# Attention scores of two heads from one 128-row product, with the keys of the pair beside zeros

## The chip, the cores and the metric

One core of one Trainium2 chip runs the whole kernel. The metric is the time of one execution in device microseconds (us). A core has five engines that run side by side, each through its own instructions in order: TensorE (PE in the profile, its weight loads as PEld), VectorE (DVE), ScalarE (ACT), GpSimd (POOL) and SyncE (SP), which here issues nearly all the DMA transfers.

## The reference

Two layers over 256 tokens of width 1024. Each layer is a gated feed-forward block (FFN), a mixer with attention, and a second FFN; each of the three is normed before and after and modulated by vectors computed from `c`.

```python
def reference(x, c, ...):
    c_act = jax.nn.silu(c)
    for l in range(DEPTH):                       # DEPTH = 2
        mod = (c_act @ ada_w[l] + ada_b[l])[:, None, :]
        sh1, sc1, g1, sh2, sc2, g2, sh3, sc3, g3 = jnp.split(mod, N_MOD, axis=-1)
        h = rmsnorm(x, norm_pre[l, 0]) * (1.0 + sc1) + sh1
        y = swiglu(h, ffn_w_gate[l, 0], ffn_w_up[l, 0], ffn_w_down[l, 0])
        x = x + 0.5 * g1 * rmsnorm(y, norm_post[l, 0])
        h = rmsnorm(x, norm_pre[l, 1]) * (1.0 + sc2) + sh2
        y = hybrid_mixer(h, mix_w_in[l], mix_b_in[l], mix_w_out[l], attn_sinks[l], group_gain[l], rel_bias)
        x = x + g2 * rmsnorm(y, norm_post[l, 1])
        ...                                      # a second FFN, as the first
    return x
```

The mixer projects `h` to queries, keys and values. Eight heads of width 64 attend within a window of 128 tokens (here "window heads": two groups of four query heads share the keys and values of one of two key heads). Eight further heads have keys and values of their own and, at 256 tokens, attend causally to all of them ("block heads"). For every head the scores are `q @ k.T * 64**-0.5` plus a bias that depends on the distance, masked; then a softmax, and the product with the values. Both groups are normed, joined and projected back.

## The kernel before

Tokens lie in two halves of 128, h = 0 and h = 1. Names that end in `_a` belong to half 0 (or an even step), in `_b` to half 1. Weights come from HBM in units of 1 MB: SP loads a unit into one of three `raw` buffers, ACT rounds it into one of six `hi` buffers (L442), DVE writes the rest, raw minus hi, into one of five `lo` buffers (L443), and PE multiplies three times (hi by hi, hi by lo, lo by hi) in a fast fp32 format: `mm3` (L481 to L483, 512 columns) and `mm3t` (here L489 to L491, 256 columns). A weight buffer is free again when PE has read it for the last time. The vectors from `c` are summed on DVE beside this (L506).

Attention itself is computed in plain fp32. One plain fp32 product is two records of PE in the trace, each with its own weight load. A mixer (`mixer`, one for each half) makes the keys and queries of the window heads from rows (transposed by `turn`, L709, into `kTw` and `qTa`), and those of the block heads with `cols_of` (L716), which writes them transposed, two heads on top of each other in the 128 partitions, into a tile of 128x512. `quad_attn` (L764) then takes four heads: two biases are loaded from a table by SP (`toeplitz`), four score products of 64 rows are issued (L778: 64 partitions of the contraction, 128 columns for half 0, 256 for half 1), into two PSUM tiles, one for the heads of the upper 64 partitions (j = 0) and one for those of the lower (j = 1):

```python
            for i in range(2):
                for j in range(2):
                    hf = slice(j * HD, (j + 1) * HD)
                    ...
                    nc.tensor.matmul(sp[j][:, i, :ncol], q_, k_, start=True, stop=True)
```

DVE adds the bias and takes the row's maximum (L783), ACT takes the exponential (L788), PE transposes it (L794), ACT copies the transposed block out of PSUM (L796), and PE multiplies it with the values (L803). In a layer and half there are four such calls, so 16 heads; over both layers 64 products of 128 columns and 64 of 256, which is 128 records of 64x128 and 64x256 in the trace (two for each of 32 heads and halves, counted by shape: 64 and 64).

The order is not that of the code: `keep_order` (L77) gathers all instructions, plays them through with its own table of costs (`cost`, L51) and priorities, and then fixes for each engine the order that came out. Weight and staging buffers go to the tiles in program order, as buffers become free. PSUM tiles of the kind `w` (`wps`) come in two buffers for each half.

Of the kernel before, what the change touches and what calls it, by code (L numbers as in the profile page):

```python
# [10 lines left out]
F32 = mybir.dt.float32  # L11
# [4 lines left out]
P = 128  # L16
# [9 lines left out]
NV = 384  # L26

NRAW, NARAW, NHI, NLO = 3, 2, 6, 5
NST, NSTR, NBIAS, NBROW, NACC, NROW = 3, 10, 3, 2, 2, 5
START_MM, START_CONV, START_CHAIN, START_SMALL = 590, 826, -286, 74  # L30
START_ORDER = ['s0 x0 s1 c0 g0 x1 c1 f0 s2 f1', 'c2 g1 f2 s3 c3 f3', '', '', '']
WARM = [2, 5, 2]
# [263 lines left out]
def trunk(ctx, tc, x, c, rel_bias, ada_w, ada_b, norm_pre, norm_post, w_gate, w_up,  # L296
# [57 lines left out]
    def ctile(shape, name, dt=F32):  # L354
        return cp.tile(shape, dt, tag=name, name=name)
# [346 lines left out]
            if (l, i) != (DEPTH - 1, 2):  # L702
                pre_norm(h, *((l, 1) if i == 0 else (l + 1, 0)))

    kTw = ctile([P, S], "kTw")
    vw = [ctile([P, P], f"vw{h}") for h in range(2)]
    kv = {}

    def turn(src, n, dst, scale):  # L709

        p_ = wps()
        for t in range(n):
            nc.tensor.transpose(p_[:, t * P:(t + 1) * P], src[:, t * P:(t + 1) * P], ident)
        nc.scalar.activation(dst, p_.rearrange("p (a b) -> p a b", a=4)[:, :n, :], AF.Copy, scale=scale)

    def cols_of(l, c0, scale):  # L716

        p_ = wps()
        w = u_cols(l, c0, 1)
        t0 = (c0 - 768) // P  # L720
        dst = stage()
        for t in range(2):
            for k in range(KT):
                mm3t(p_[:, t * 256:(t + 1) * 256], k, w, slice(t * P, (t + 1) * P), k == 0, k == KT - 1)
            nc.scalar.activation(dst[:, t * 256:(t + 1) * 256], p_[:, t * 256:(t + 1) * 256], AF.Identity,
                                 scale=scale, bias=bq[:, l, t0 + t:t0 + t + 1])
        return dst

    def mixer(h, l):

        nk = 1 + h
        toks = slice(h * P, (h + 1) * P)

        def brow(c0, n):
            return bcast(b_in[l:l + 1, c0:c0 + n], n)


        p_ = wps()
        w = u_cols(l, 512, 2)
        for k in range(8):  # L740
            mm3(p_[:, :256], hT[0][:, h, k, :], hT[1][:, h, k, :], w, k, slice(0, 256), k == 0, k == 7)
        b_ = brow(512, 256)
        ks = st()
        nc.vector.tensor_add(ks[:, :P], p_[:, :P], b_[:, :P])
        nc.vector.tensor_add(vw[h], p_[:, P:256], b_[:, P:])
        turn(ks, 1, kTw[:, toks].rearrange("p (o t) -> p o t", o=1), 1.0)

        p_ = wps()
        rows_of(h, [p_], [lambda q: u_in(l, 0, q)])
        qs = st()  # L750
        nat = lambda t: t.rearrange("p (j i d) -> p j i d", j=2, i=4)
        nc.vector.tensor_tensor(qs.rearrange("p (i j d) -> p j i d", i=4, j=2), nat(p_), nat(brow(0, 512)), op=ALU.add)
        qTa = stage()
        turn(qs, 4, qTa.rearrange("p (a b) -> p a b", a=4), 0.125)
        yield

        p_ = wps()
        rows_of(h, [p_], [lambda q: u_in(l, 1792, q)])
        kv["v", h] = stage()
        nc.vector.tensor_add(kv["v", h], p_, brow(1792, 512))  # L760

        negm, lsum = tiny(16, f"negm{h}"), tiny(16, f"lsum{h}")

        def quad_attn(i0, swa, acc):  # L764

            head = (lambda j, i: 4 * j + i) if swa else (lambda j, i: 8 + 2 * i + j)
            ncol = nk * P
            bt = [toeplitz(head(j, i0), head(0, 1) - head(0, 0), ncol) for j in range(2)]
            sp = [wps().rearrange("p (i k) -> p i k", i=2) for _ in range(2)]
            for i in range(2):  # L770
                for j in range(2):
                    hf = slice(j * HD, (j + 1) * HD)
                    if swa:
                        q_, k_ = qTa[hf, (i0 + i) * P:(i0 + i + 1) * P], kTw[hf, :ncol]
                    else:
                        q_ = kv["q", i0 // 2][hf, i * 256 + h * P:i * 256 + (h + 1) * P]
                        k_ = kv["k", i0 // 2][hf, i * 256:i * 256 + ncol]
                    nc.tensor.matmul(sp[j][:, i, :ncol], q_, k_, start=True, stop=True)  # L778
            s = [st().rearrange("p (a b) -> p a b", a=2) for _ in range(2)]
            for j in range(2):  # L780
                for i in range(2):
                    hd_ = head(j, i0 + i)
                    nc.vector.tensor_tensor_reduce(s[j][:, i, :ncol], sp[j][:, i, :ncol], bt[j][:, i, :ncol], -1.0,  # L783
                                                   nsink[:, l, hd_:hd_ + 1] if swa else 3.0e38, ALU.add, ALU.min,
                                                   negm[:, hd_:hd_ + 1])
                for i in range(2):
                    hd_ = head(j, i0 + i)
                    nc.scalar.activation(s[j][:, i, :ncol], s[j][:, i, :ncol], AF.Exp, scale=-1.0, bias=negm[:, hd_:hd_ + 1],  # L788
                                         accum_out=lsum[:, hd_:hd_ + 1])
                tp = wps()  # L790
                for i in range(2):
                    for b in range(nk):
                        t = i * nk + b
                        nc.tensor.transpose(tp[:, t * P:(t + 1) * P], s[j][:, i, b * P:(b + 1) * P], ident)  # L794
                pT = st()
                nc.scalar.activation(pT[:, :2 * ncol], tp[:, :2 * ncol], AF.Copy)  # L796
                for i in range(2):
                    hd_ = head(j, i0 + i)
                    vc = j * HD if swa else (hd_ - 8) * HD
                    oc = (hd_ % 8) * HD  # L800
                    for b in range(nk):
                        t = i * nk + b
                        nc.tensor.matmul(acc[:, oc:oc + HD], pT[:, t * P:(t + 1) * P], (vw[b] if swa else kv["v", b])[:, vc:vc + HD],  # L803
                                         start=b == 0, stop=b == nk - 1)

        def group_out(g, acc):
            hs = slice(g * 8, g * 8 + 8)
            if g == 0:
                e = tiny(8, f"es{h}")
                nc.vector.tensor_add(e, sinkb[:, l, :], negm[:, hs])  # L810
                nc.scalar.activation(e, e, AF.Exp)
                nc.vector.tensor_add(lsum[:, hs], lsum[:, hs], e)
            rl = tiny(8, f"rl{h}")
            nc.vector.reciprocal(rl, lsum[:, hs])
            y = st()
            nc.vector.tensor_tensor(y.rearrange("p (a b) -> p a b", a=8), acc.rearrange("p (a b) -> p a b", a=8),
                                    rl.rearrange("p (a o) -> p a o", o=1).to_broadcast([P, 8, HD]), op=ALU.mult)
            ss = tiny(1, f"ssg{h}")
            nc.scalar.activation(junk, y, AF.Square, scale=512.0 ** -0.5, accum_out=ss)
            r2 = rstd_of(ss, None, "rstdg")  # L820
            y2 = st()
            nc.vector.scalar_tensor_tensor(y2, y, r2, bcast(group_gain[l:l + 1, g * 512:(g + 1) * 512], 512),
                                           op0=ALU.mult, op1=ALU.mult)
            to_T(h, g * 4, 4, y2)

        yield
        acc0 = aps(h)
        quad_attn(0, True, acc0)
        yield
        quad_attn(2, True, acc0)  # L830
        yield
        acc1 = aps(h)
        quad_attn(0, False, acc1)
        yield
        group_out(0, acc0)
        yield
        quad_attn(2, False, acc1)
        yield
        group_out(1, acc1)
        yield  # L840
        accs = [aps(h), aps(h)]
        for u in range(4):
            w = u_out(l, u)
            for n in range(2):
                for k in range(2):
                    kt = u * 2 + k
                    mm3(accs[n], hT[0][:, h, kt, :], hT[1][:, h, kt, :], w, k, slice(n * 512, (n + 1) * 512),
                        kt == 0, kt == 7)
        yield
        post_norm(h, l, 1, accs)  # L850
        pre_norm(h, l, 2)

    def mix(l):
        steps = [mixer(h, l) for h in range(2)]

        def go(h):
            cur[0] = h
            next(steps[h], None)

        for step in sec["mix"]:  # L860
            if step < "2":
                go(int(step))
            else:
                cur[0] = 0
                g = int(step) - 2
                kv["k", g] = cols_of(l, 1280 + g * 256, 1.0)
                kv["q", g] = cols_of(l, 768 + g * 256, 0.125)


    def first_srcs(q):  # L870
# [156 lines left out]
```

## Time and profile before

| | |
|---|---|
| time, median of 3 runs | 1036.47 us (1036.47 to 1038.14) |
| the profiled execution | 1035.72 us, of which its span 1033.9 us from the first to the last instruction |
| PE busy, share of the span | 98%, 6578 products |
| PE weight loads | 87% |
| DVE, ACT, POOL busy | 78%, 53%, 4% |
| DMA | 263.9 MB through SP's queue, 76% of 16 engines' span |

The span is the profiled execution's own; 1.8 us lie around it. A record of PE has a start that was measured and an end that is modelled, and records overlap: how long PE takes for one is read from its start to the start of the next. The two attention stretches lie at about 230 to 330 us (layer 0) and 725 to 830 us (layer 1), the FFNs in between and around them.

### The profile page before, as it was taken

How to read it: one execution, taken by the hardware profiler on the slowest of the kernel's cores; microseconds unless marked ns; L12 is line 12 of the kernel's file. 1: busy time of each engine (PE TensorE's matmuls, PEld its weight loads, DVE VectorE, ACT ScalarE, POOL GpSimd, SP SyncE). 2: the span in 40 equal slices, each digit the busy share in tenths (PEclk: the TensorE clock that was granted, in tenths of full speed). 3: DMA queues.
4: the chain of work that ended last, by engine and by line, in shares of the span. 5: the costliest groups of instructions: out<-in, count | busy, mean ns of one | idle time of the engine just before them, and what ended most of it. 6: DMA issues, size and time to landing. Idle time of an engine off the chain costs nothing.

```text
span 1033.9 us, 17402 instructions
## 1 busy us (share of the span) xinstructions
PE 1017.8 (98%) x6578; PEld 902.0 (87%) x6578; DVE 802.2 (78%) x1493; ACT 546.3 (53%) x1238; POOL 38.4 (4%) x74
## 2 busy tenths in 40 slices
PE   8999999999999999999999999999999999999997
PEld 3699998978888899999979999998888879999996
DVE  4799887988887998888888988786878698554542
ACT  2456434565667655556465445454566666444431
POOL 1000000020001000000010000000000110000000
PEclk9999999999999999999999999999999999999999
DMA  9999999969885587989838998885688647556511
GB/s 328 362 350 325 319 306 362 333 212 285 309 287 167 190 302 258 319 291 311 285 121 293 324 315 302 281 305 182 201 298 279 186 150 262 204 168 200 174 71 41
DMA packets 173919, 265.10 MB, mean 256 GB/s; under 512 B 6412, under 2 KB 109548, under 8 KB 173836
## 3 DMA queue, kind: packets, MB, share of 16 engines
q1 hardware_dynamic: 173680, 263.93, 76.0%
q8 instruction: 51, 0.84, 0.3%
q14 instruction: 32, 0.26, 0.1%
q10 hardware_dynamic: 156, 0.07, 0.0%
HBM read 262.90 MB, written 4.22 MB: 258 GB/s over the span
## 4 chain that ended last, share of the span: by engine, by line
issue 56%; PE 33%; DMA 4%; DVE 3%; POOL 2%; ACT 1%; SPq 1%; POOLq 0%; DVEq 0%; ACTq 0%
PE w_a L489 3%; PE w_a L491 3%; PE w_a L490 3%; PE a_b L481 2%; PE a_b L482 2%; PE a_b L483 2%; DMA raw_a<-in_ffn_w_up_dram 2%; PE w_b L778 2%; PE a_b L803 1%; PE a_a L481 1%; PE a_a L482 1%; PE a_a L483 1%; PE w_a L778 1%; DMA araw_a<-in_ada_w_dram 1%; PE w_b L482 1%
## 5 line engine op out<-in xcount | busy, mean ns | idle before, releaser
L443 DVE TENSOR_TENSOR lo_a<-raw_a,hi_a 128x512 fp32r<-128x512 f32 (+1 forms) x540 | 294.2, 594 | 48.9 <-issue 23.4
L442 ACT ACTIVATE hi_a<-raw_a 128x512 fp32r<-128x512 f32 (+1 forms) x540 | 259.5, 547 | 129.9 <-DMA raw_a<-in_ffn_w_up_dram 26.1
L489 PE MATMUL w_a<-hTh,hi_a 128*128 128x256 f32 x768 | 218.7, 285 | 1.1 <-ACT hi_a L442 1.1
L490 PE MATMUL w_a<-hTl,hi_a 128*128 128x256 f32 x768 | 217.6, 284 | 0.0
L491 PE MATMUL w_a<-hTh,lo_a 128*128 128x256 f32 x768 | 217.5, 284 | 0.0
L489 PEld LDWEIGHTS w_a<-hTh,hi_a 128*128 128x128 f32 x768 | 147.2, 192 | 2.4 <-ACT hi_a L442 1.3
L490 PEld LDWEIGHTS w_a<-hTl,hi_a 128*128 128x128 f32 x768 | 147.2, 192 | 0.8
L491 PEld LDWEIGHTS w_a<-hTh,lo_a 128*128 128x128 f32 x768 | 146.9, 192 | 0.3
L490 PE MATMUL w_b<-hTl,hi_b 128*128 128x256 f32 x512 | 145.0, 283 | 0.0
L489 PE MATMUL w_b<-hTh,hi_b 128*128 128x256 f32 x512 | 144.9, 283 | 0.0
L491 PE MATMUL w_b<-hTh,lo_b 128*128 128x256 f32 x512 | 144.8, 283 | 0.0
L443 DVE TENSOR_TENSOR lo_b<-raw_b,hi_b 128x512 fp32r<-128x512 f32 (+1 forms) x224 | 120.3, 590 | 24.7 <-issue 17.5
L442 ACT ACTIVATE hi_b<-raw_b 128x512 fp32r<-128x512 f32 (+1 forms) x224 | 105.6, 544 | 64.0 <-PE w_b L490 27.0
L489 PEld LDWEIGHTS w_b<-hTh,hi_b 128*128 128x128 f32 x512 | 98.1, 192 | 1.1
L490 PEld LDWEIGHTS w_b<-hTl,hi_b 128*128 128x128 f32 x512 | 98.1, 192 | 0.9
L491 PEld LDWEIGHTS w_b<-hTh,lo_b 128*128 128x128 f32 x512 | 98.0, 192 | 0.2
L506 DVE SCALAR_TENSOR_TENSOR acc_a<-araw_a,ccol,acc_a 128x512 f32<-128x512 f32 x110 | 82.4, 749 | 7.8 <-DMA araw_a<-in_ada_w_dram 6.2
L482 PE MATMUL a_b<-lo_a,str_a 128*128 128x512 f32 x156 | 60.8, 392 | 0.0
L483 PE MATMUL a_b<-hi_a,str_a 128*128 128x512 f32 x156 | 60.4, 390 | 0.0
L481 PE MATMUL a_b<-hi_a,str_a 128*128 128x512 f32 x156 | 59.7, 391 | 0.0
L506 DVE SCALAR_TENSOR_TENSOR acc_b<-araw_b,ccol,acc_b 128x512 f32<-128x512 f32 x46 | 34.5, 749 | 7.9 <-DMA araw_b<-in_ada_w_dram 7.1
L481 PE MATMUL w_a<-hi_a,hTh 128*128 128x512 f32 (+1 forms) x96 | 36.1, 378 | 0.6 <-DVE hTl L591 0.6
(240 smaller groups left out, 1732.7 us busy)
## 6 DMA issues: line engine op xcount, KB each, us to landing
araw_a<-in_ada_w_dram SPq DMA_DIRECT2D x84, 512.0 KB
raw_a<-in_ffn_w_down_dram SPq DMA_DIRECT2D x30, 1024.0 KB
raw_a<-in_ffn_w_gate_dram SPq DMA_DIRECT2D x26, 1024.0 KB
raw_a<-in_ffn_w_up_dram SPq DMA_DIRECT2D x26, 1024.0 KB
araw_b<-in_ada_w_dram SPq DMA_DIRECT2D x44, 512.0 KB
raw_a<-in_mix_w_in_dram SPq DMA_DIRECT2D x18, 1024.0 KB
raw_b<-in_ffn_w_gate_dram SPq DMA_DIRECT2D x16, 1024.0 KB
raw_b<-in_ffn_w_up_dram SPq DMA_DIRECT2D x16, 1024.0 KB
```

Source lines behind the costliest of these rows:

```text
L442: nc.scalar.activation(hi[:, sl], raw[:, sl], AF.Copy)
L443: nc.vector.tensor_sub(lo[:, sl], raw[:, sl], hi[:, sl].bitcast(F32))
L481: nc.tensor.matmul(ps_, hh, wh, start=start, stop=False)
L482: nc.tensor.matmul(ps_, hh, wl, start=False, stop=False)
L483: nc.tensor.matmul(ps_, hl, wh, start=False, stop=stop)
L489: nc.tensor.matmul(ps_, wh, hh, start=start, stop=False)
L490: nc.tensor.matmul(ps_, wh, hl, start=False, stop=False)
L491: nc.tensor.matmul(ps_, wl, hh, start=False, stop=stop)
L506: nc.vector.scalar_tensor_tensor(acc[:, :n], raw[:, t, :], ccol[:, k:k + 1], b if t == 0 else acc[:, :n], op0=ALU.mult, op1=ALU.add)
L778: nc.tensor.matmul(sp[j][:, i, :ncol], q_, k_, start=True, stop=True)
L803: nc.tensor.matmul(acc[:, oc:oc + HD], pT[:, t * P:(t + 1) * P], (vw[b] if swa else kv["v", b])[:, vc:vc + HD], start=b == 0, stop=b == nk ...
```

## The change

The score products of a pair of heads become one product of 128 rows. The keys of the pair stand in a tile with two column blocks for each pair: in the first block the 64 upper partitions hold the keys of head j = 0 and the lower are zero, in the second the lower hold those of j = 1 and the upper are zero. The queries of both heads (128 partitions) are the stationary operand, both blocks (256 or 512 columns) move, and the result has the scores of both heads side by side in one PSUM tile. The rest of the attention then goes pair by pair. The zeros of the window heads' tile `kzw` are written once at the start; the block heads' tile is taken from the pool of `hi` buffers in each layer, and POOL writes its zeros there each time. ACT writes the keys in two halves. The staging pool `str` goes from 10 buffers to 9. Line numbers of the changed kernel are higher by 17 in its attention: the products of the scores stand at L796, the transposes at L811, the value products at L820.

```diff
-NST, NSTR, NBIAS, NBROW, NACC, NROW = 3, 10, 3, 2, 2, 5
+NST, NSTR, NBIAS, NBROW, NACC, NROW = 3, 9, 3, 2, 2, 5
...
-    kTw = ctile([P, S], "kTw")
+    kzw = ctile([P, 2, S], "kzw")
+    nc.gpsimd.memset(kzw[HD:, 0, :], 0.0)
+    nc.gpsimd.memset(kzw[:HD, 1, :], 0.0)
...
-    def cols_of(l, c0, scale):
+    def cols_of(l, c0, scale, dst):
...
-            nc.scalar.activation(dst[:, t * 256:(t + 1) * 256], p_[:, t * 256:(t + 1) * 256], AF.Identity,
-                                 scale=scale, bias=bq[:, l, t0 + t:t0 + t + 1])
-        return dst
+            for rows_, to in dst(t):
+                nc.scalar.activation(to, p_[rows_, t * 256:(t + 1) * 256], AF.Identity,
+                                     scale=scale, bias=bq[rows_, l, t0 + t:t0 + t + 1])
+
+    def keys_of(l, g):
+
+        if g == 0:
+            t = phi.tile([P, 2048], F32, tag="hi", name=nm("kz"))
+            kv["k"] = t.rearrange("p (i j n) -> p i j n", i=4, j=2)
+            nc.gpsimd.memset(kv["k"][HD:, :, 0, :], 0.0)
+            nc.gpsimd.memset(kv["k"][:HD, :, 1, :], 0.0)
+        kz = kv["k"]
+        cols_of(l, 1280 + g * 256, 1.0, lambda t: [(slice(j * HD, (j + 1) * HD), kz[j * HD:(j + 1) * HD, g * 2 + t, j, :])
+                                                   for j in range(2)])
...
-        turn(ks, 1, kTw[:, toks].rearrange("p (o t) -> p o t", o=1), 1.0)
+        kt_ = turn(ks, 1)
+        for j in range(2):
+            hf = slice(j * HD, (j + 1) * HD)
+            nc.scalar.activation(kzw[hf, j, toks], kt_[hf, :], AF.Copy)
...
-            bt = [toeplitz(head(j, i0), head(0, 1) - head(0, 0), ncol) for j in range(2)]
-            sp = [wps().rearrange("p (i k) -> p i k", i=2) for _ in range(2)]
-            for i in range(2):
+            for i in range(i0, i0 + 2):
+                bt = toeplitz(head(0, i), head(1, 0) - head(0, 0), ncol)
+                sp = wps()[:, :2 * ncol].rearrange("p (j k) -> p j k", j=2)
+                if swa:
+                    q_, k_ = qTa[:, i * P:(i + 1) * P], kzw[:, :, :ncol]
+                else:
+                    q_ = kv["q", i // 2][:, i % 2 * 256 + h * P:i % 2 * 256 + (h + 1) * P]
+                    k_ = kv["k"][:, i, :, :ncol]
+                nc.tensor.matmul(sp, q_, k_, start=True, stop=True)
...
```

On PE, in layer 0, where half 0 finishes its window heads and half 1 begins, these rows stand before (about 260 to 263 us of the trace; `w_a`, `w_b` are PSUM tiles of the halves, `st` the exponentials, `vw` the values):

```order
L803 MATMUL a_a_2685<-vw_132,st_a_2705 128x64
L794 MATMUL w_a_2713<-ident,st_a_2697 128x128
L778 MATMUL w_a_2724<-kTw,str_a_2513 128x128 x2
L794 MATMUL w_a_2713<-ident,st_a_2697 128x128
L483 MATMUL w_b_2654<-hi_a_2547,hTl 128x512
L523 MATMUL w_a_2840<-ast_a_2841,onesr 128x512
L524 MATMUL w_a_2840<-ast_a_2842,onesr 128x512
L778 MATMUL w_a_2725<-kTw,str_a_2513 128x128
L803 MATMUL a_a_2685<-vw_132,st_a_2716 128x64 x2
L778 MATMUL w_a_2725<-kTw,str_a_2513 128x128
L794 MATMUL w_a_2736<-ident,st_a_2730 128x128
```

At the same place of the changed kernel:

```order
L820 MATMUL a_a_2689<-vw_134,st_a_2718 128x64 x2
L523 MATMUL w_a_2845<-ast_a_2846,onesr 128x512
L811 MATMUL w_a_2731<-ident,st_a_2726 128x128
L796 MATMUL w_a_2740<-kzw,str_a_2516 128x256
L811 MATMUL w_a_2731<-ident,st_a_2726 128x128
L524 MATMUL w_a_2845<-ast_a_2847,onesr 128x512
L796 MATMUL w_b_2918<-kzw,str_b_2651 128x512
L820 MATMUL a_a_2689<-vw_134,st_a_2734 128x64 x2
L811 MATMUL w_a_2747<-ident,st_a_2742 128x128
```

The 64-row products, of which several stand scattered between others there, and in twos where both write the same PSUM tile, are gone; one product a pair stands between the transposes of the pair before it.

On POOL, at the end of the first FFN of layer 1, these rows stand before (`rstd` are the reciprocal norms, first of half 0 and then of half 1):

```order
L577 TENSOR_SCALAR rstd_a_7859<-ss_a_7856 128x1
L579 TENSOR_TENSOR rstd_a_7860<-rstd_a_7859,mhalf 128x1
L577 TENSOR_SCALAR rstd_a_7872<-ss_a_7869 128x1
L579 TENSOR_TENSOR rstd_a_7873<-rstd_a_7872,mhalf 128x1
L577 TENSOR_SCALAR rstd_b_7935<-ss_b_7932 128x1
L579 TENSOR_TENSOR rstd_b_7936<-rstd_b_7935,mhalf 128x1
```

At the same place of the changed kernel:

```order
L577 TENSOR_SCALAR rstd_a_7865<-ss_a_7862 128x1
L579 TENSOR_TENSOR rstd_a_7866<-rstd_a_7865,mhalf 128x1
L736 MEMSET kz_a_8279 64x4x256
L737 MEMSET kz_a_8279 64x4x256
L577 TENSOR_SCALAR rstd_b_7928<-ss_b_7925 128x1
L579 TENSOR_TENSOR rstd_b_7929<-rstd_b_7928,mhalf 128x1
```

The two writes of zeros stand ahead of the norm of half 1, and in layer 0 likewise. Outside the mixers and the places next to them the rows of PE stand as before.

## Rows read from the trace of the kernel before

**Rows 1.** Busy us by stretch: length, sum, PE, PEld, DVE, ACT, POOL, ...

```profile
240.00:325.00 85.00, 85.00 (x545) 72.24 (x544) 69.01 (x166) 54.60 (x152) 4.51 (x8) 1.00 0.88 288
740.00:822.00 82.00, 82.00 (x526) 68.44 (x525) 62.36 (x152) 54.17 (x145) 3.07 (x6) 1.00 0.83 274
350.00:500.00 150.00, 150.00 (x1041) 140.42 (x1040) 131.94 (x309) 86.03 (x250) 0.00 (x0) 1.00 0.89 299
```

**Rows 2.** Timeline of PE, layer 0: start us, us, engine, line, operation, tiles, shape, count

```profile
297.20 0.28 PE L490 MATMUL w_a<-hTl,hi_a 128*128 128x256 f32 x1
297.32 1.00 PE L803 MATMUL a_b<-vw,st_b 128*128 128x64 f32 x8
298.16 0.39 PE L794 MATMUL w_b<-ident,st_b 128*128 128x128 f32 x2
298.48 1.13 PE L778 MATMUL w_b<-str_a,str_a 64*128 64x256 f32 x4
299.54 0.44 PE L794 MATMUL w_b<-ident,st_b 128*128 128x128 f32 x2
...
300.76 0.28 PE L490 MATMUL w_a<-hTl,hi_a 128*128 128x256 f32 x1
300.97 0.70 PE L778 MATMUL w_b<-str_a,str_a 64*128 64x256 f32 x2
301.60 0.66 PE L803 MATMUL a_b<-vw,st_b 128*128 128x64 f32 x4
302.07 0.36 PE L491 MATMUL w_a<-hTh,lo_a 128*128 128x256 f32 x1
...
304.02 0.71 PE L778 MATMUL w_a<-str_a,str_a 64*128 64x128 f32 x4
304.66 0.66 PE L803 MATMUL a_a<-str_a,st_a 128*128 128x64 f32 x4
```

**Rows 3.** Timeline of PE, runs of 64-row products: the first, the sixes, the last

```profile
246.07 0.71 PE L778 MATMUL w_a<-kTw,str_a 64*128 64x128 f32 x4
...
264.12 1.14 PE L778 MATMUL w_b<-kTw,str_b 64*128 64x256 f32 x6
265.19 0.66 PE L803 MATMUL a_a<-vw,st_a 128*128 128x64 f32 x4
...
813.21 1.13 PE L778 MATMUL w_b<-str_a,str_a 64*128 64x256 f32 x4
```

**Rows 4.** Timeline of PE at the start: plain fp32 products, 128 rows, 512 columns

```profile
6.33 4.56 PE L916 MATMUL a_b<-x,ident 128*128 128x512 f32 x10
```

**Rows 5.** POOL timeline: a write of 128 columns; the norm of half 1, layer 1

```profile
0.72 0.20 POOL L899 MEMSET str_a<- 128x128 f32 x1 [0.29 <-POOLq L1008]
...
725.09 0.30 POOL L577 TENSOR_SCALAR rstd_b<-ss_b 128x1 f32<-128x1 f32 x1 [4.73 <-ACT junk L616]
```

**Rows 6.** Layer 1, end of the first FFN: timelines of PE and DVE

```profile
723.81 0.39 PE L483 MATMUL a_b<-hi_a,str_a 128*128 128x512 f32 x1
...
729.92 0.75 DVE L609 SCALAR_TENSOR_TENSOR st_b<-st_b,rstd_b,row_a 128x512 f32<-128x512 f32 x1 [0.84 <-POOL rstd_b L579]
...
730.73 0.66 PE L588 MATMUL w_b<-ident,st_b 128*128 128x128 f32 x4
```

**Rows 7.** ACT's writes of keys and queries by shape: busy us, mean ns | idle before

```profile
L725 ACT ACTIVATE str_a<-w_a,bq 128x256 f32<-128x256 f32 x16 | 7.4, 471 | 12.4 <-PE w_a L491 12.3
```

**Rows 8.** A weight unit of layer 0: ACT's rounding, and PE's first product with it

```profile
238.32 2.19 ACT L442 ACTIVATE hi_a<-raw_a 128x512 fp32r<-128x512 f32 x4
...
265.72 0.36 PE L489 MATMUL w_a<-hTh,hi_a 128*128 128x256 f32 x1
```

**Rows 9.** The chain behind a score product: DVE by shape, ACT and PE timelines

```profile
L783 DVE CUSTOM_DVE_ANT_0 st_a<-w_a,bias_a,nsink 128x128 f32<-128x128 f32 x16 | 5.0, 348 | 1.0 <-PE w_a L778 0.5 <-PE w_b L483 0.4
...
754.23 0.39 ACT L788 ACTIVATE st_a<-st_a,negm_a 128x128 f32<-128x128 f32 x1
...
754.68 0.27 PE L794 MATMUL w_a<-ident,st_a 128*128 128x128 f32 x1
```

More of the change, by code (lines that the diff above doesn't have):

```diff
@@ L703, in ffn, with turn @@
                 pre_norm(h, *((l, 1) if i == 0 else (l + 1, 0)))
-    kTw = ctile([P, S], "kTw")
+    kzw = ctile([P, 2, S], "kzw")
+    nc.gpsimd.memset(kzw[HD:, 0, :], 0.0)
+    nc.gpsimd.memset(kzw[:HD, 1, :], 0.0)
     vw = [ctile([P, P], f"vw{h}") for h in range(2)]
     kv = {}
-    def turn(src, n, dst, scale):
+    def turn(src, n):
         p_ = wps()
@@ L713, in turn @@
             nc.tensor.transpose(p_[:, t * P:(t + 1) * P], src[:, t * P:(t + 1) * P], ident)
-        nc.scalar.activation(dst, p_.rearrange("p (a b) -> p a b", a=4)[:, :n, :], AF.Copy, scale=scale)
-    def cols_of(l, c0, scale):
+        return p_[:, :n * P]
+    def cols_of(l, c0, scale, dst):
         p_ = wps()
@@ L720, in cols_of @@
         t0 = (c0 - 768) // P
-        dst = stage()
         for t in range(2):
@@ L724, in cols_of, with queries_of @@
                 mm3t(p_[:, t * 256:(t + 1) * 256], k, w, slice(t * P, (t + 1) * P), k == 0, k == KT - 1)
-            nc.scalar.activation(dst[:, t * 256:(t + 1) * 256], p_[:, t * 256:(t + 1) * 256], AF.Identity,
-                                 scale=scale, bias=bq[:, l, t0 + t:t0 + t + 1])
-        return dst
+            for rows_, to in dst(t):
[10 more added lines that the diff above has]
+                                                   for j in range(2)])
+    def queries_of(l, g):
+        kv["q", g] = stage()
+        cols_of(l, 768 + g * 256, 0.125, lambda t: [(slice(0, P), kv["q", g][:, t * 256:(t + 1) * 256])])
     def mixer(h, l):
@@ L753, in mixer @@
         qTa = stage()
-        turn(qs, 4, qTa.rearrange("p (a b) -> p a b", a=4), 0.125)
+        nc.scalar.activation(qTa, turn(qs, 4), AF.Copy, scale=0.125)
         yield
@@ L767, in quad_attn @@
             ncol = nk * P
-            bt = [toeplitz(head(j, i0), head(0, 1) - head(0, 0), ncol) for j in range(2)]
-            sp = [wps().rearrange("p (i k) -> p i k", i=2) for _ in range(2)]
-            for i in range(2):
-                for j in range(2):
[L772 to L783, printed above, removed]
+            for i in range(i0, i0 + 2):
[7 more added lines that the diff above has]
+                nc.tensor.matmul(sp, q_, k_, start=True, stop=True)
+                s = st()[:, :2 * ncol].rearrange("p (j k) -> p j k", j=2)
+                for j in range(2):
+                    hd_ = head(j, i)
+                    nc.vector.tensor_tensor_reduce(s[:, j, :], sp[:, j, :], bt[:, j, :ncol], -1.0,
@@ L784, in quad_attn @@
                                                    nsink[:, l, hd_:hd_ + 1] if swa else 3.0e38, ALU.add, ALU.min,
                                                    negm[:, hd_:hd_ + 1])
-                for i in range(2):
-                    hd_ = head(j, i0 + i)
-                    nc.scalar.activation(s[j][:, i, :ncol], s[j][:, i, :ncol], AF.Exp, scale=-1.0, bias=negm[:, hd_:hd_ + 1],
+                for j in range(2):
+                    hd_ = head(j, i)
+                    nc.scalar.activation(s[:, j, :], s[:, j, :], AF.Exp, scale=-1.0, bias=negm[:, hd_:hd_ + 1],
@@ L789, in quad_attn @@
                                          accum_out=lsum[:, hd_:hd_ + 1])
                 tp = wps()
-                for i in range(2):
+                for j in range(2):
                     for b in range(nk):
-                        t = i * nk + b
-                        nc.tensor.transpose(tp[:, t * P:(t + 1) * P], s[j][:, i, b * P:(b + 1) * P], ident)
+                        t = j * nk + b
+                        nc.tensor.transpose(tp[:, t * P:(t + 1) * P], s[:, j, b * P:(b + 1) * P], ident)
@@ L795, in quad_attn @@
                 pT = st()
                 nc.scalar.activation(pT[:, :2 * ncol], tp[:, :2 * ncol], AF.Copy)
-                for i in range(2):
-                    hd_ = head(j, i0 + i)
+                for j in range(2):
+                    hd_ = head(j, i)
                     vc = j * HD if swa else (hd_ - 8) * HD
@@ L801, in quad_attn @@
                     for b in range(nk):
-                        t = i * nk + b
+                        t = j * nk + b
                         nc.tensor.matmul(acc[:, oc:oc + HD], pT[:, t * P:(t + 1) * P], (vw[b] if swa else kv["v", b])[:, vc:vc + HD],
@@ L865, in mix @@
                 g = int(step) - 2
-                kv["k", g] = cols_of(l, 1280 + g * 256, 1.0)
-                kv["q", g] = cols_of(l, 768 + g * 256, 0.125)
+                keys_of(l, g)
+                queries_of(l, g)
     def first_srcs(q):
```

## The prediction, made before the changed kernel was run

> **What bounds the kernel now.** I read the busy time by stretch first, to see which engine is full where the change is. In both attention stretches PE is busy all the time, 85.00 of 85 and 82.00 of 82 us, and so it is in an FFN stretch (150.00 of 150); the granted clock is 1.00 in all three, the upper level of 2.4 GHz [rows 1]. DVE has 69.0 of 85 (81%), 62.4 of 82 (76%) and, in the FFN, 131.9 of 150 (88%); the DMA queues are at 0.88, 0.83 and 0.89. So PE sets the pace, and in the FFN it does so while DVE is busier than it is in the attention. But "busy" counts modelled ends that overlap. What a product costs PE shows only in the steps from one start to the next, so I went to PE's timeline next.
>
> There the steady step of a 256-column product of the projections is 0.12 us (297.20 to 297.32, where a plain fp32 product of 128 rows follows it, which therefore costs nothing to enter) [rows 2]. Around the 64-row score products the steps are longer than the columns explain:
> - the last product ahead: 300.76 to 300.97 is 0.21 in place of 0.12, so +0.09;
> - the run: four records take 298.48 to 299.54 = 1.06, two take 300.97 to 301.60 = 0.63. A further record costs (1.06 - 0.63)/2 = 0.215, so two records are worth 0.43 and 0.20 comes on top of each run. For 128 columns, four records in 304.02 to 304.66 = 0.64, less the 0.20, give 0.11 each;
> - the value products behind: four in 301.60 to 302.07 = 0.47. Eight of them take 297.32 to 298.16 = 0.84, so four are 0.42, and +0.05 remains.
>
> One visit of PE to 64-row products thus costs 0.09 + 0.20 + 0.05 = 0.34 us beyond its columns. Transposes and value products are plain fp32 too, with 128 rows, and pay nothing on entry; I take the price to belong to the 64 rows. PE's timeline has 42 such runs, 20 in layer 0 and 22 in layer 1, the first at 246.07, the last at 813.21 [rows 3]. They hold 128 records, 64 for each width.
>
> **The change, part by part.**
>
> Removed: 42 visits of 0.34 = 14.3 us. Two of them were cheaper: in the runs of six (the one at 264.12, and one like it in layer 1) six records and the visit would be 6 x 0.215 + 0.20 = 1.49, but 264.12 to 265.19 is 1.07 [rows 3]. Two records ran beside two others and saved 0.42 each time. The change loses these 0.84. Together -14.3 + 0.84 = -13.5 (rounded).
>
> Streaming, before: 64 x 0.215 + 64 x 0.11 = 20.8 us. After: 64 records become 32 of 512 columns and 64 become 32 of 256; zeros move like keys. By columns that is 32 x 0.43 + 32 x 0.215 = 20.6, no difference. The nearest row of a plain 128-row product of 512 columns is ten in 4.56 us, 0.456 each with the last one's end [rows 4], which gives at most 32 x 0.026 = +0.8. I take 0; were the new records as cheap as the two overlapped ones of the sixes, the sum would be 20.8 - 32 x 0.42 = 7 at its very least, but there is nothing left to overlap with, since each fills all 128 rows.
>
> The Trainium skill ("TensorE: Matmul & The Clock Gate", the table under "Why this matters for your kernels") says the opposite of this change: products with a small contraction at different partitions run side by side, started within about 4 ns. This trace shows that in the two sixes alone; in the fours the records stand 0.215 apart, since the order puts two of the same half of the partitions and the same PSUM tile next to each other. By the rule, with all of them side by side, the streaming before would be 10.4 and the change would bring 13.5 - 10.4 = 3 us less the terms below; by the rows it was never had, so the sum goes by the rows.
>
> Added, entry cost: each new score product is entered from another kind of product. The 0.12 of 297.20 says nothing; the +0.05 behind a visit says 32 x 0.05 = 1.6 over the 32 pairs. I take 0.5 (range 0 to 1.6).
>
> Added, a shorter chain: the bias and maximum on DVE, the exponential on ACT, the transposes on PE, the copy on ACT and the value products now run pair by pair. A pair's chain from its score product on is two DVE passes of 0.348, and 0.45 from an exponential's start (754.23) to the transposes that read it (754.68) [rows 9]. In the new order there stand one or two projection or value products of another half between a score product and its transposes in most places, but little in some (at the place shown in the PE rows, the transposes of the pair before, one product that sums, the score product of the other half and two value products). Where PE arrives early it waits for the rest of that chain. Some 15 groups in two layers look tight; by the visit's own size, 0.34, each would lose 0.1 on average and at most 0.34: 1.5 taken, 0 to 5 as bounds.
>
> Added, ACT: the keys go out in two halves of 64 partitions. A write costs by its columns, so each of the 8 key writes of 0.471 becomes two [rows 7], +3.8 us, and four writes of the window heads' keys double as well, at most as long each, +1.9. ACT then has about 57 of 85 and 57 of 82 us; hidden behind PE, since the keys' next reader comes tens of products later. Were it not hidden, a last half-write ahead of a score product costs 0.47, inside the chain's bounds above.
>
> Added, POOL: two writes of zeros in each layer, 1024 columns each. The nearest row has 128 columns in 0.20 [rows 5], so one is between 0.20 (no dearer) and 1.6 (by columns); 0.9 taken, 1.8 for the two. They wait for a weight buffer that is free when PE has read it for the last time in the FFN, about 724.2 (723.81 + 0.39) [rows 6]. Then they run to 726.0, while the norm of half 1 behind them on POOL began at 725.09 [rows 5]: 0.9 late (0 to 2.3). Who waits: DVE's scaling by that norm ends at 730.67 (729.92 + 0.75), and PE's transposes start at 730.73 right behind it [rows 6]. In layer 1 PE therefore loses up to 0.9. PE may use a part of it for other products it has there, so I take 0.5 for both layers, up to 2.4.
>
> Moved: one `hi` buffer in six serves the keys during a mixer, and staging has nine buffers. The rounding of a unit began at 238.32 and PE's first use of it was at 265.72, 27 us later [rows 8], so a start later by several us is covered. If it isn't, the price is the third rival's. The biases are as many loads, on SP at slightly other places.
>
> Sum: -13.5 + 0 + 0.5 + 1.5 + 0.5 = -11.0 us. The profiled execution took 1035.72 (span 1033.9 and 1.8 around it), which gives 1024.7. It lay 0.75 below the median of 1036.47; against that median the forecast is 1025.4.
>
> **Rivals.**
> 1. The 0.34 is paid for each visit to a score product of any height. Then 32 new visits cost 32 x 0.34 = 10.9 of the 13.5, and 2.6 less the 2.5 added leaves nothing: about 1036. For it: no row before shows a 128-row score product. Against: value products and transposes, the same kind with 128 rows, enter freely at 297.32 [rows 2]. Chance 0.05.
> 2. Slower: the pair's chain. PE is faster now, and a pair offers half the cover of a quad. This decides from 13.5/32 = 0.42 us lost per pair on. With 0.6 per pair (the chain of 2 x 0.348 + 0.45 = 1.15, with half of it uncovered) 19.2 are lost: -13.5 + 19.2 + 1.0 = +6.7, 1043. For it: 0.45 from exponential to transposes without a gap [rows 9]. Against: two halves interleave, and the projections stand between. Chance 0.07.
> 3. The weights: DVE must write `lo` at a higher rate when PE runs through the stretch 5 to 7 us faster: 69/78 = 88%, the share of the FFN. If it falls behind by the missing buffer, half the gain is waited away: 1030 to 1031. For it: the DMA share of 0.88 would rise to 0.88 x 85/78 = 0.96. Against: in the FFN PE runs its steady step at that DVE share [rows 1]. Chance 0.10.
> 4. More: shorter steps also close other gaps of PE in the two stretches, and neither chain nor POOL costs anything; with some 2 us on top of the full 13.5 this is 1020 to 1021. Chance 0.06.
>
> **How the numbers follow.** The forecast has the remaining 0.72, with its own range 1021 to 1029: the added terms reach from 0 to about +4 beyond what is taken, and less than 3 below. Below lies rival 4, above rival 3, and so the range for 8 in 10 is 1019 to 1033; it leaves out rivals 1 and 2 and the outer ends of the chain's bounds. A measurement of this kernel can tell about 0.2%, 2 us. Faster by more: forecast, rivals 3 and 4, 0.72 + 0.10 + 0.06 = 0.88. Within: rival 1, 0.05. Slower: rival 2, 0.07.
>
> **What would show it.** In the new profile, PE's timeline should have score records of 128x512 with steps of about 0.43 and of 128x256 with 0.215, no excess of 0.09 ahead and 0.05 behind, and both attention stretches some 5 to 7 us shorter. If rival 1 holds, the excess is there on 128 rows. If rival 2, transposes follow ACT's exponentials at once in most pairs, with steps of 0.6 and more ahead of them. If rival 3, a weight product starts when DVE's `lo` write ends. POOL's two writes should show their own length, with the norm of half 1 behind them by the time named. The forecast is wrong if the steps before the transposes add up to more than 5 us, or if the new records cost clearly more than their columns.

## The result and the profile after

| | before | after |
|---|---|---|
| median, first comparison | 1036.47 us, 4 runs, 1036.20 to 1038.14 | 1027.78 us, 4 runs, 1026.31 to 1029.76; ratio 0.9914 [0.9893, 0.9935] |
| second and third comparison | 1036.94 and 1036.99 us | 1029.25 and 1028.14 us, 6 runs each; ratios 0.9919 [0.9899, 0.9939] and 0.9912 [0.9893, 0.9931] |
| profiled execution | 1035.72 us, span 1033.9 | 1029.76 us, span 1027.6 |

The change makes the kernel 8 to 9 us faster, about 0.85%. Forecast were 11.0 us less and 1025.4 us, with a range from 1019 to 1033.

Busy time by stretch in the changed kernel (columns as in [rows 1]; behind POOL stand the granted clock, the DMA share and GB/s):

```profile
240.00:325.00 85.00, 84.56 (x547) 73.66 (x546) 74.00 (x175) 62.11 (x167) 3.90 (x8) 1.00 0.90 308
740.00:822.00 82.00, 81.18 (x521) 69.47 (x519) 66.94 (x158) 59.74 (x157) 4.33 (x8) 1.00 0.84 282
350.00:500.00 150.00, 150.00 (x1050) 140.88 (x1049) 132.29 (x308) 87.12 (x252) 0.00 (x0) 1.00 0.87 296
```

PE is no longer busy without a gap in the attention stretches, DVE and ACT do more in the same time, the granted clock is 1.00 as before. The place on PE that answers to [rows 2] (start, length, operation, count):

```profile
300.64 0.38 PE L811 MATMUL w_b<-ident,st_b 128*128 128x128 f32 x2
300.86 1.02 PE L796 MATMUL w_b<-kz_a,str_a 128*128 128x512 f32 x2
301.72 0.38 PE L811 MATMUL w_b<-ident,st_b 128*128 128x128 f32 x2
301.94 1.00 PE L820 MATMUL a_b<-vw,st_b 128*128 128x64 f32 x8
302.77 0.28 PE L811 MATMUL w_a<-ident,st_a 128*128 128x128 f32 x1
302.89 0.60 PE L796 MATMUL w_a<-kz_a,str_a 128*128 128x256 f32 x2
303.32 0.27 PE L811 MATMUL w_a<-ident,st_a 128*128 128x128 f32 x1
```

Two records of 512 columns take 300.86 to 301.72 = 0.86, two of 256 take 302.89 to 303.32 = 0.43: the columns and nothing else. The transposes ahead keep their 0.11 each (300.64 to 300.86), the value products behind too (0.83 for eight). Where the price of the old visits lay is seen in the weight loads. Before (line 778):

```profile
300.65 0.19 PEld L490 LDWEIGHTS w_a<-hTl,hi_a 128*128 128x128 f32 x1
300.97 0.29 PEld L778 LDWEIGHTS w_b<-str_a,str_a 64*128 64x128 f32 x2
301.60 0.30 PEld L803 LDWEIGHTS a_b<-vw,st_b 128*128 128x128 f32 x2 [0.33 <-issue]
```

After (line 796):

```profile
300.54 0.25 PEld L811 LDWEIGHTS w_b<-ident,st_b 128*128 128x128 f32 x2
300.75 0.30 PEld L796 LDWEIGHTS w_b<-kz_a,str_a 128*128 128x128 f32 x2
```

The load of the 64 rows starts with its own product at 300.97, and the next load of 128 rows at 301.60 with its own; the new load starts at 300.75, 0.11 ahead of its product, while PE still multiplies. In all 42 runs of before, the first load of 64 rows and the load of 128 rows behind the run start within 4 ns of their products. The Trainium skill ("TensorEngine Tiling (Array Packing)", Key Properties) states: "Changing tiling mode (not just tile) drains the TensorE". This trace agrees for the change between 64 and 128 rows, and gives the price that the page does not: 0.3 us and more for a visit. That the array drains is the page's word; what the trace shows is that the loads no longer run ahead.

Summed over all records (32 products of each width, two records each; the 64 of each width named for the kernel before are the records): in the kernel before, the runs of 64-row products had 7.4 us inside, 4.2 on the product ahead and 2.7 on the one behind beyond their columns, 14.3 together. In the changed kernel it is -0.2. The time from each product's start to the next one's, summed by line between the same two weight products (two stretches, from the last FFN products ahead of a mixer to the FFN behind it; lines of before), worked out from the starts of all PE records:

| us, both layers | before | after | second profile | third profile |
|---|---|---|---|---|
| all | 327.56 | 317.72 | 318.87 | 317.97 |
| scores (778) | 28.23 | 18.64 | 18.63 | 18.64 |
| transposes and values (794, 803) | 31.77 | 28.35 | 29.95 | 29.20 |
| 524 in layer 1 | 1.62 | 3.20 | 3.19 | 3.20 |
| all other lines | 265.94 | 267.53 | 267.10 | 266.93 |

So the mixers gave 9.8, 8.7 and 9.6 us, against 14.3 + 0.2 of visits removed: some 5 us were added. (The scores' 18.6 are under 20.6 because behind eight of the pairs the next product starts 0.2 to 0.4 early, 0.03 after the second record; its own step is longer by as much. In 3.20 of line 524 there is one such 0.4.) What was added is seen best in layer 1, first on POOL, DVE and PE in turn:

```profile
721.97 0.95 POOL L736 MEMSET kz_a<- 64x1024 f32 x1 [3.97 <-issue]
722.97 0.94 POOL L737 MEMSET kz_a<- 64x1024 f32 x1
724.01 0.30 POOL L577 TENSOR_SCALAR rstd_b<-ss_b 128x1 f32<-128x1 f32 x1
...
725.00 1.41 DVE L624 SCALAR_TENSOR_TENSOR x<-st_b,rstd_b,x 128x512 f32<-128x512 f32 x2 [1.60 <-POOL rstd_b L579]
...
726.67 0.33 PE L716 MATMUL w_a<-ident,st_a 128*128 128x128 f32 x1 [1.48 <-DVE st_a L761]
```

The two writes of zeros take 0.95 and 0.94, the norm of half 1 starts 0.10 behind them, DVE waits 1.60 for it, and PE 1.48 for a tile that stands behind that on DVE (it is booked on line 524, the product ahead). Before, PE waited 0.20 at this place, so 1.3 are new:

```profile
727.73 0.33 PE L713 MATMUL w_a<-ident,st_a 128*128 128x128 f32 x1 [0.20 <-DVE st_a L744]
```

In layer 0 the same place cost PE 0.2 us at most. Second, PE arrives early at transposes; the largest such wait in layer 1:

```profile
749.36 0.40 PE L483 MATMUL w_b<-hi_a,hTl 128*128 128x512 f32 x1
750.27 0.33 PE L811 MATMUL w_a<-ident,st_a 128*128 128x128 f32 x1 [0.52 <-ACT st_a L805]
```

The step from 749.36 is 0.91 in place of 0.23, 0.7 for an exponential that ACT had not finished. It is there in this profile alone. All three have 0.7 at 803 us, for a copy and an exponential of ACT (the second has 0.5 more there, for DVE). The second and the third have one wait of 1.0 and 0.9 in layer 0. Before, the list of PE's waits between 742 and 830 us is empty.

The three waits that one profile alone has begin with a transfer. An engine that works in order stood waiting for it, and what PE needed stood behind: on DVE in the first profile, ahead of the pair's maximum; on ACT in the second, ahead of a write of queries; on DVE in the third, for the biases of half 1. From the three profiles:

```profile
748.01 0.75 DVE L506 SCALAR_TENSOR_TENSOR acc_a<-araw_a,ccol,acc_a 128x512 f32<-128x512 f32 x1 [1.54 <-DMA araw_a<-in_ada_w_dram]
...
293.96 0.63 ACT L442 ACTIVATE hi_a<-raw_a 128x512 fp32r<-128x512 f32 x1 [1.66 <-DMA raw_a<-in_mix_w_out_dram]
...
284.88 0.48 DVE L800 CUSTOM_DVE_ANT_0 st_b<-w_b,bias_b,nsink 128x256 f32<-128x256 f32 x1 [2.02 <-DMA bias_b<-scr]
```

In the second profile the first of these transfers was late too (1.03), and PE did not wait behind it. Before, DVE waited for such units as well (2.2 us between 715 and 845), with no wait of PE for an exponential.

Beside the mixers, PE lost time in layer 0's first FFN, ahead of all that the change touches. The wait in the changed kernel, with ACT's wait for the weight unit to land ahead of it, and the same wait of PE in a second profile of the kernel before:

```profile
165.25 2.19 ACT L442 ACTIVATE hi_a<-raw_a 128x512 fp32r<-128x512 f32 x4 [8.01 <-DMA raw_a<-in_ffn_w_up_dram]
...
165.93 0.39 PE L489 MATMUL w_a<-hTh,hi_a 128*128 128x256 f32 x1 [3.39 <-ACT hi_a L442]
```

```profile
166.14 0.58 PE L489 MATMUL w_a<-hTh,hi_a 128*128 128x256 f32 x1 [4.28 <-ACT hi_a L442]
```

In the first profile of before it was 1.1. Single profiles of two kernels are therefore compared here only between fixed products, and the whole by medians.

### The profile page after: what moved, and what is told of

Its sections match the earlier page's. It is cut to its first block, busy times and chain, and to the rows that moved or that the text cites. A ratio compares the mean times of both kernels' runs of the same rounds, so it can differ in the third digit from the quotient of the medians.

```text
span 1027.6 us, 17311 instructions
## 1 busy us (share of the span) xinstructions
PE 1007.1 (98%) x6514; PEld 895.9 (87%) x6514; DVE 800.6 (78%) x1493; ACT 552.9 (54%) x1250; POOL 41.3 (4%) x80
```

## The experiments

**The same kernels again.** Is the wait at 163 us the change's?

> The changed kernel once more. In its profile PE lost 3.8 us more than the kernel before at 163 us, in the first FFN, waiting for a weight unit, outside all that the change touches; two of its four runs were 1026.3 and 1027.0, two 1028.6 and 1029.8. Theory A (this wait is chance, of the transfers): another profile has it shorter or elsewhere, and the median is 1026 to 1028. Theory B (it comes with the new order of transfers or the POOL writes at the start): the same wait stands at 163 us again, 3 us or more.

Median 1029.25 (1025.49 to 1031.40). The wait is there again, 2.6 us; in the third profile it is 3.8. The median is above theory A's 1026 to 1028 and the wait under theory B's 3, so this run alone decides nothing.

> The kernel before, for a second profile of it. Theory A (the wait of PE for a weight unit at 163 us varies by chance, since SP's order up to there is the same in both kernels): it is longer than the 1.1 us of the first profile in this one, or the spread of the times, 1035 to 1040, shows it. Theory B (it is longer only in the changed kernel): about 1 us again.

1036.98 (1034.88 to 1041.70), ratio 1.0001 [0.9986, 1.0017]; the wait is 4.28. Theory A: it varies in either kernel, from 1.1 to 4.3 in five profiles. In all five ACT waited for the same unit to land, 6.4 to 8.3 us. Between the fixed products around the mixers the two profiles of before differ by 0.2 us.

**Two products of 64 rows a pair**, into two PSUM tiles. Is it the rows, or the new order?

```
-                sp = wps()[:, :2 * ncol].rearrange("p (j k) -> p j k", j=2)
+                sp = [wps()[:, :ncol] for _ in range(2)]
...
-                nc.tensor.matmul(sp, q_, k_, start=True, stop=True)
+                for j in range(2):
+                    hf = slice(j * HD, (j + 1) * HD)
+                    nc.tensor.matmul(sp[j], q_[hf, :], k_[hf, j, :], start=True, stop=True)
```

> The changed kernel, pair by pair and with the zeros, but each pair's scores again from two products of 64 rows into two PSUM tiles. Theory A (the price is that of the 64 rows, 0.34 us a visit): the order has 64 products in about 55 visits, 55 x 0.34 = 18.7, less what adjacent products of different halves save by running side by side (about 9 pairs, 0.2 to 0.4 each, 3), so 15 us slower than the changed kernel, near 1043. Theory B (the gain came from going pair by pair and from the new order): within 2 us of the changed kernel, near 1028.

1050.74, ratio 1.0123 [1.0103, 1.0143]. Theory B is out. A's size was too low: 54 visits cost 21.4 us beyond their columns, 0.40 each, what some neighbours saved by running side by side taken off. The mixers took 22 us more than those of the changed kernel, so next to nothing is left for the order. PE's timeline shows visits in close succession:

```profile
265.48 0.70 PE L798 MATMUL w_b<-kzw,str_b 64*128 64x256 f32 x2
266.11 0.33 PE L813 MATMUL w_a<-ident,st_a 128*128 128x128 f32 x1
266.37 0.48 PE L798 MATMUL w_a<-kzw,str_a 64*128 64x128 f32 x2
266.78 0.33 PE L813 MATMUL w_b<-ident,st_b 128*128 128x128 f32 x1
267.04 0.49 PE L798 MATMUL w_a<-kzw,str_a 64*128 64x128 f32 x2
```

A single transpose between two of them takes 0.26 (266.11 to 266.37) in place of 0.11: it pays on both sides.

**One product more, of 64 or of 128 rows.** The price by itself; `HD` is 64, and the second run has `P`, 128, in its place:

```
+                nc.tensor.matmul(sp[:, 0, :64], q_[:HD, :], k_[:HD, 0, :64], start=True, stop=True)
                 nc.tensor.matmul(sp, q_, k_, start=True, stop=True)
```

> The changed kernel with one further product ahead of each pair's scores: 64 rows, 64 columns, into the place that the scores then overwrite. 32 products, two records each. Theory A (0.34 us a visit to 64 rows): 32 x (0.34 + 2 x 0.055) = 14.4 us more, near 1042. Theory B (64 rows cost no more than others): the columns alone, 32 x 0.11 = 3.5 us more, near 1031.

> As the run before, the further product with 128 rows and the same 64 columns. Both theories: the columns alone, 32 x 0.11 = 3.5 us more than the changed kernel, near 1031, so that the difference to the run with 64 rows is the price of the 64 rows: 10.9 us by theory A, 0 by theory B.

1044.06 (1042.77 to 1045.31) and 1034.72 (1032.25 to 1039.17): 9.3 us between them, 0.29 a visit; theory A, whose 10.9 was a little high. The same place in the two timelines, first with 64 rows, then with 128:

```profile
277.13 0.60 PE L812 MATMUL w_b<-ident,st_b 128*128 128x128 f32 x4
277.66 0.43 PE L796 MATMUL w_b<-kzw,str_b 64*128 64x64 f32 x2
278.03 1.12 PE L797 MATMUL w_b<-kzw,str_b 128*128 128x512 f32 x2
```

```profile
275.84 0.60 PE L812 MATMUL w_b<-ident,st_b 128*128 128x128 f32 x4
276.27 0.33 PE L796 MATMUL w_b<-kzw,str_b 128*128 128x64 f32 x2
276.44 1.08 PE L797 MATMUL w_b<-kzw,str_b 128*128 128x512 f32 x2
```

The step of the transposes is 0.53 against 0.43, that of the extra product 0.37 against 0.17, and the scores behind take 0.56 against 0.52: 0.34 in all at this place, the price of the prediction. The run with 128 rows was 5.5 us over the changed kernel of the same comparison (1029.25), not 3.5: its second record steps 0.11, as a transpose of 128 columns does, and the scores behind begin with a step that is 0.055 longer (0.485 for 512 columns, 0.272 for 256). Why so short a record costs this was not tested.

**The zeros later.** One column copied from half 1's window keys ahead of the writes:

```
+            nc.scalar.activation(kv["k"][:, 0, 0, :1], kzw[:, 0, S - 1:], AF.Copy)
+            nc.scalar.activation(kv["k"][:, 0, 1, :1], kzw[:, 0, S - 1:], AF.Copy)
             nc.gpsimd.memset(kv["k"][HD:, :, 0, :], 0.0)
```

> The changed kernel with POOL's zeros in a later place: a copy of one column from the window keys of half 1, ahead of them in each layer, makes them wait until half 1's keys are there. In layer 1 of the changed kernel DVE waits 1.60 us for the norm of half 1, which stands behind the two writes of 0.95 us on POOL, where it waited 0.32 before, and PE waits 1.48 behind DVE. Theory A (the place of the zeros costs this): these two waits go back, 1.3 us less than the changed kernel, near 1027.5 where it has 1028.8, within what can be told apart only in the trace. Theory B (PE waits there for something else): the wait of PE at 726 us stays over 1 us.

1028.08, ratio 0.9915 [0.9898, 0.9931]. PE's and DVE's wait went as theory A has it (DVE waits for nothing that is shown, PE 0.38 in place of 1.48):

```profile
724.92 1.42 DVE L624 SCALAR_TENSOR_TENSOR x<-st_b,rstd_b,x 128x512 f32<-128x512 f32 x2
...
726.77 0.33 PE L716 MATMUL w_a<-ident,st_a 128*128 128x128 f32 x1 [0.38 <-DVE st_a L763]
```

But layer 1's stretch gave 4.2 us against before, where the changed kernel's three profiles gave 3.9, 4.0 and 4.7: what was won at this place did not come out of the stretch. The wait is caused by the zeros; that it costs the end 1.3 us is not shown.

**64 rows side by side.** The order got a rule more: the score products of a call follow each other on PE, and both PSUM tiles must be free at the first. Once with the kernel before, four products a call (e6, e9), once with the two products of a pair (e7).

```
+    for g in together:
+        ks = [at[n] for n in g]
+        for k in ks[1:]:
...
+            alloc[ks[0]] += alloc[k]
+        tails += ks[1:]
```

> The kernel before (64-row products, four heads at a time, no zeros), with one rule more in the order: the four score products of a quad follow each other on PE, heads of the upper and the lower 64 partitions in turn, into two PSUM tiles. In the run with two products of 64 rows a pair, such neighbours started 6 or 7 ns apart and four records of 128 columns took 0.42 us. Theory A (they run side by side, and a visit costs 0.34): 16 visits in place of 42 save 8.8 us, and half the streaming goes, 10.4 less the 0.8 that two runs had; 18 us less than before, less up to 8 us for waiting until both PSUM tiles are free: 1018 to 1027, faster than the changed kernel. Theory B (side by side only in the starts, the PSUM writes one after the other): streaming stays, 16 visits save 8.8 less the waits: 1028 to 1034.

1026.14 (1024.36 to 1029.28), ratio 0.9900 [0.9883, 0.9918]: faster than before by 10.9, at the far end of theory A's range.

```profile
300.20 1.14 PE L795 MATMUL w_b<-str_a,str_a 64*128 64x256 f32 x8
301.26 0.66 PE L821 MATMUL a_b<-vw,st_b 128*128 128x64 f32 x4
301.85 0.72 PE L795 MATMUL w_a<-str_a,str_a 64*128 64x128 f32 x8
302.49 0.55 PE L821 MATMUL a_b<-vw,st_b 128*128 128x64 f32 x3
```

Eight records of 256 columns take 1.06, what four took in [rows 2]; eight of 128 take 0.64, as four did. Side by side is real, and the scores fell from 28.2 us to 14.4. But the two profiles gave only 12.9 and 10.1 us in the mixers, of the 18 by columns and visits. A part of the rest is waits of PE for the chain. The largest three, of 4.6 us in layer 0 in e9 (total, times, longest):

```profile
PE w_a L812 <- ACT st_a L806: 1.9, 2, 1.1
PE w_b L604 <- DVE st_b L625: 0.9, 1, 0.9
PE w_b L729 <- DVE st_b L768: 0.7, 1, 0.7
```

> The run with two products of 64 rows a pair (e2), with the two products made to follow each other directly on PE. Theory A (side by side, 0.34 a visit): 32 visits cost 10.9 us, the streaming falls from 20.6 to 10.3, so it comes out with the changed kernel, within 2 us of it (1027 to 1031). Theory B (no gain from neighbours beyond the starts): 10.9 us more than the changed kernel, near 1040.

1034.86 (1033.18 to 1037.03), ratio 0.9983 [0.9971, 0.9994], 6 us over the changed kernel, between the theories. Its scores take 17.9 us and the edges of 29 runs 5.1, 23.0 against 20.4 (18.6 and 1.8) in the changed kernel: 2.6 of the 6. The rest stays open; waiting for both PSUM tiles was not separated.

> The kernel of quads side by side (e6) once more, in one call with the changed kernel. Theory A (it beats the changed kernel): the ratio of both to the kernel before differs as in the runs so far, 0.990 against 0.992, so 2 to 3 us less than the changed kernel, 1025 to 1027. Theory B (the difference was chance, of the wait at 163 us): within 1 us of it.

> The changed kernel for the third time, as the measure of the run before in this call: 1027.5 to 1029.5.

1027.24 (ratio 0.9900 [0.9883, 0.9917]) and 1028.14 (0.9912 [0.9893, 0.9931]). Over both comparisons the quads' 11 runs have the median 1026.8, the changed kernel's 16 have 1028.6. In the last comparison the quads lie 0.9 us under the changed kernel, within theory B's 1 us, and the intervals of the ratios overlap: the quads are better than before for certain; that they are better than the changed kernel is not shown.

## Why the prediction was right

- **What bounds.** Right. PE sets the pace: what was taken from its steps came out of the time, but for 5 us. The stretches were to be 5 to 7 us shorter; layer 0 gave 5.9, 4.6 and 4.9 in the three profiles, layer 1 only 3.9, 4.0 and 4.7.
- **42 visits, 0.34 each, 64 rows.** Right in place, cause and size: 14.3 us found, overlaps of the sixes included, where the sum had 13.5. The extra products put 0.29 on a visit by the medians and 0.34 by the steps of one, the run with close visits 0.40, so 0.34 is no constant: a neighbour that is itself between two visits pays twice.
- **Streaming.** Right: steps of 0.43 and 0.215. The Trainium skill's rule on products side by side, weighed in the prediction, did not touch this change, since the order before had hardly used it; e6 shows that it holds where the order lets it, with starts of 6 to 7 ns apart and not the about 4 that the prediction gives from it.
- **Entry cost.** Set at 0.5, is 0.
- **ACT.** Right; the halves of 64 partitions cost as the whole had. They were hidden, but for the wait of 1.0 in the second profile, where a write of queries stood behind a late weight unit:

```profile
L728 ACT ACTIVATE kz_a<-w_a,bq 64x256 f32<-64x256 f32 x16 | 7.5, 469 | 4.9 <-PE w_a L491 4.5
L728 ACT ACTIVATE str_a<-w_a,bq 128x256 f32<-128x256 f32 x8 | 3.8, 471 | 0.5 <-PE w_a L491 0.4
```

- **POOL.** The write was set at 0.9 and took 0.95, and the norm behind it came late as named. The way from there to PE is another one: the norm that begins at 725.09 is not the one that the scaling at 729.92 reads, but the one ahead of it. DVE waits for it in line 624, and PE for line 761, which does not read the norm and only stands behind it in DVE's order. PE lost 1.3 there, not 0.5; by e5 the end gets little of it back.
- **The pair's chain.** Set at 1.5; the largest waits (749 and 803 us, and one in layer 0) make 1.4, 2.2 and 1.6 us in the three profiles. The size fits in part by luck: 0.7, 1.0 and 0.9 of them begin with a late transfer, for which the sum had no term. With POOL's 1.3 that is 2.7 to 3.5 of the 5 us added; the rest, spread over the other lines, is not assigned. No run varied the staging pool or the `hi` buffer that the keys take.
- **What was off in size** is thus the sum of the added terms: 2.5 by the prediction, 5 by the profiles, most of it by POOL and by what no term was set up for. The 2.5 between them are as large as the 2.4 us between the forecast and the first median. The visits taken away were 0.8 more than in the sum, which hid a part of it.
- **Rivals.** The first is out by the new records and by e4. The second's wait exists, at under 0.1 a pair and not 0.6. The third did not come as written: no wait of PE in the mixers is for a `lo` write, and the DMA share rose to 0.90 to 0.92 in layer 0, not 0.96. But late transfers did cost PE 0.7 to 1.0 us in each profile, by way of engines that work in order. The fourth did not come.

## What to carry to other kernels

Read PE by the steps between starts, ahead of and behind a product too: a product that changes the row tiling can cost more at its edges than its columns do, and zeros that fill the rows can be cheaper, as here, where they cost PE nothing. Where such products stay, let those of different rows stand side by side and in long runs, and see what the order makes of the code. When PE gets faster, expect a part of the gain to come back as waits, here 5 of 14.5 us; follow each wait back to its first cause, which was a transfer in three of the large ones, and look at what stands in order on the engine in between.

## What the runs showed of the hardware

Two 64-row products at different partitions into different PSUM tiles start 6 to 7 ns apart in most cases (5 to 8 in e6, once 13 in e2; the records of the two). After the wait of 3.39 us at 163 us the granted clock was not full for a moment, so the wait cost more than its own length:

```profile
165.00:170.00 5.00, 4.07 (x21) 4.08 (x22) 4.09 (x7) 2.19 (x4) 0.00 (x0) 0.66 0.95 341
...
167.00:168.00 1.00, 1.00 (x6) 1.00 (x6) 1.00 (x3) 0.44 (x1) 0.00 (x0) 0.50 0.89 305
```

PE began again at 165.93. Over the five us the mean is 0.66, in the one from 167 it is 0.50, which is the lower of the two levels (1.2 and 2.4 GHz); in the stretches ahead and behind it is 1.00. From 166.4 to 169.8 us a product of 256 columns steps 0.21 in place of 0.12, and that makes 1.6 us on top of the wait.
